# Hybrid attention and HGRN2 block: all attention values in one job of 512 columns, and two other jobs moved forward

## The chip, the core and the metric

The kernel runs on one core of a Trainium2 chip. The time is device microseconds of one launch: the median of three runs of the kernel before is 1435.72 us (1435.06 to 1435.78). Five engines with queues of their own work side by side: TensorE (PE in the profile, with its weight loads as PEld), VectorE (DVE), ScalarE (ACT), GpSimd (POOL) and SyncE (SP), which issues most of the DMAs. Each executes its list of instructions in order and waits for the others where a tile demands it.

## The reference

One layer on x of 1024 tokens by 1024 columns, in float32. After an RMS norm, one projection `w_in` gives everything that the two branches need:

```python
xn = rmsnorm(x, norm1_g[layer])
u = xn @ w_in[layer].astype(f32)
q_sb, k_sb, v_sb, f_raw, i_hg, q_hg, g_hg, gate_sb, gate_hg = jnp.split(u, list(c), axis=-1)
o_sb = stick_breaking_attention(split_heads(q_sb, SB_HEADS), ...)      # 8 heads of 64
f = lb + (1.0 - lb) * jax.nn.sigmoid(f_raw)
k_hg = (1.0 - lb) * jax.nn.sigmoid(-f_raw)
o_hg = hgrn2_chunkwise(silu(q_hg), k_hg, i_hg, log(f))                 # 4 heads of 128
o_hg = rmsnorm(o_hg, hg_norm_g) * jax.nn.silu(g_hg)
merged = g_a * (o_sb @ w_o_sb) + g_b * (o_hg @ w_o_hg)                 # g_a, g_b: sigmoids of the gates
h = x + merged @ w_out
h = h + jnp.square(jax.nn.relu(rmsnorm(h, norm2_g) @ w_ff1)) @ w_ff2
return rmsnorm(h, final_g)
```

Stick-breaking attention is strictly causal: the weight of key s for query t is sigmoid(z_ts) times the product of (1 - sigmoid(z_tj)) over the keys j between s and t. HGRN2 is a linear recurrence over tokens, S_t = diag(f_t) S_(t-1) + k_t v_t, with the output S_t' q_t.

## The kernel before, in words

**Products.** Every float32 product is made of three matmuls on pairs: an operand is split into hi (a rounded copy, by ScalarE as a CAST) and lo (the rest, by VectorE as a subtraction, L161); `three` (L553) issues hi by hi, hi by lo and lo by hi into one PSUM bank. A `Unit` holds one piece of weights: `load` fetches it, `split` makes hi and lo.

**Jobs and lanes.** Projections are jobs of a `Stream` (`st`, L487): a job is a list of steps of a few matmuls, in the order in which the jobs were added. `st.advance(n, upto)` issues n further steps, but none beyond job `upto`; `st.finish(upto)` issues all up to there. Starting a job also splits the next one's weights and loads those of the one after it. TensorE's instructions lie on two lanes, "main" (the steps of the attention and of HGRN2, which depend on other engines) and "fill" (the stream's steps). Within these orders a scheduler places the instructions of each engine, in view of the pools of tiles (`slots` of 1024 columns, `halves` of 512, raw and split weights, eight PSUM banks).

**Stages.**
1. Head: norm of x and transposes to `xn` (`xnt`) in two halves of tokens, among them the first job (`first_job`, L728), which makes q and k of head 0 (`pjqk`) and V of heads 0 to 3 (`pjv0`), 256 columns wide, one piece for each of eight token blocks.
2. Attention: 64 items, eight heads by eight query blocks in the order 7, 0, 6, 1, 5, 2, 4, 3. Each item has scores (`z`, TensorE, then two sigmoids on ScalarE), weights (a scan and a product on VectorE, tiles `rm` and `bt`, L802 and L169), a turn (`pw`, transposes of the weights, split to hi and lo) and values (`po`). After each item the stream goes on by its share of `n_fill` = 126 steps, up to job `j_att`. The jobs are q and k of heads 1 to 7, V of heads 4 to 7 (`v_job(1)`, behind head 4), f and q of the HGRN2 heads (`pjf`, `pjq`), and two raw output-gate jobs (`raw_job`, KT and KT+1).
3. HGRN2: for each of four heads `hg_levels(h)` (L1006), which yields eight times, and `hg_tail(h)` (L1131), six times; the tail of head h-1 runs in turns with the levels of head h. In the levels, VectorE makes products of k and q (the pair sums `sd`, `sl` of levels 0 and 1, through `pairs_of` and `sums_of`), multiplies k and q by the decay of a level (tile `pp`), and lays the scores of a level (`sl`) into `sc` with predicated copies (L1051, L1122). Levels 2 to 4 take their scores from k and q in 16 matmuls, levels 5 and 6 in many small ones. The tail transposes k (`pk`), makes the states (`pkv`, and a chain of seven updates of k on VectorE, L1159 and L1161), the outputs (`pho`), their norm (squares on ScalarE, a power on POOL, a product `hon` on VectorE) and transposes (`pot`).
4. The gates (`gX`, `gY`: TensorE's products with summed operands `gs`), the output product, the MLP.

The loop of stage 3, where the order of the fill is set:

```python
    FILL = (3.4, 2.2, 2.8, 2.9, 2.9)
        upto = (j_i, j_raw[1], j_raw[6], j_sb[1], j_sb[2])[h]
                if next(g, StopIteration) is not StopIteration:
                    owed += FILL[h]
                    st.advance(int(owed), upto)
                    owed -= int(owed)
```

`upto` is a job: the fill of head 0 goes up to the job of i (`pji`), that of head 3 up to the second, and the last turn's (h = 4, only the tail of head 3) up to the third of the four jobs `j_sb`, the products of the attention's output with `w_o_sb` (`pys`). What is left of these is finished behind the loop.

Of the kernel before, what the change touches and what calls it, by code (L numbers as in the profile page):

```python
# [9 lines left out]
F32 = mybir.dt.float32  # L10
F32R = mybir.dt.float32r
# [8 lines left out]
P = 128  # L20
T = 1024
# [18 lines left out]
def kernel(  # L40
# [86 lines left out]
    def matmul(*a, **k):  # L127
        return pe(nc.tensor.matmul(*a, **k))  # L128
# [449 lines left out]

    def token_steps(name, unit, acts, tbs, epilogue, lo_last=False, n=256):

        pk = 1024 // n
        for tb in tbs:
            ps = bank(f"{name}_{tb}")[:, 0:n]
            for lo in (False, True) if lo_last else (None,):
                for kt in range(KT):
                    sh, sl = acts.stat(kt, tb)
                    wh, wl = unit.hl[kt // pk]
                    cs = slice((kt % pk) * n, (kt % pk + 1) * n)
                    if lo is None:
                        three(ps, sh, sl, wh[:, cs], wl[:, cs], kt == 0, kt == KT - 1)  # L590
                        if kt < KT - 1 and kt % pk == pk - 1:
                            yield
                    elif lo:
                        matmul(ps, sh, wl[:, cs], start=False, stop=kt == KT - 1)
                    else:
                        matmul(ps, sh, wh[:, cs], start=kt == 0, stop=False)
                        matmul(ps, sl, wh[:, cs], start=False, stop=False)
                if lo is False:
                    yield
            epilogue(ps, tb)  # L600
            yield

    def wide_unit(name, mat, c0, n=256):
# [56 lines left out]

    def v_epilogue(quad):


        def ep(ps, tb):
            if tb % 2 == 0:
                vt[quad, tb // 2] = slot(f"V{quad}_{tb // 2}", F32R)
            V = vt[quad, tb // 2].rearrange("p (t h s d) -> p t h s d", t=2, h=4, s=2)
            src = ps.rearrange("p (h d) -> p h d", h=4)
            hi_lo(V[:, tb % 2, :, 0, :], V[:, tb % 2, :, 1, :], src)

        return ep

# [4 lines left out]
    def qk_epilogue(h):  # L677
# [12 lines left out]
        return ep  # L690

    def v_unit(quad):
        return wide_unit(f"wv{quad}", W_IN, C_V + quad * 256)

    def v_job(quad):
        unit = v_unit(quad)
        return st.add(
            [unit], lambda: token_steps(f"pjv{quad}", unit, xn, range(NT), v_epilogue(quad))
        )

# [27 lines left out]
    def first_job():  # L728
        name, u_qk, ep = qk_item(0)
        u_qk.__class__ = FirstUnit  # L730
        u_v = v_unit(0)

        def body():
            v_ep = v_epilogue(0)
            for half, parts in enumerate((((0, 2), (2, 2)), ((0, 4),))):
                ps = bank(f"{name}_{half}")
                for b0, n in parts:
                    ts = slice(b0 * P, (b0 + n) * P)
                    yield from proj_half(ps[:, ts], u_qk.hl[0], xn.mov, KT, half, ts=ts)
                    if b0 + n == 4:  # L740
                        ep(ps, half)
                    if half == 0 and b0 > 0:
                        st.prefetch()
                    tb = 4 * half + b0
                    yield from token_steps("pjv0", u_v, xn, range(tb, tb + n), v_ep, tb == 0)

        return st.add([u_qk], body), u_qk, u_v

    j_first, u_qk0, u_v0 = first_job()
# [256 lines left out]
    def hg_levels(h):  # L1006
# [16 lines left out]

        def pairs_of(name, n, *products):

            t, h_, l_ = (slot_n(f"{name}_{x}", n, d) for x, d in zip("xhl", (F32, F32R, F32R)))
            for (a, b, w), (i, cs) in zip(products, halves()):
                x = mul(t[:, cs].rearrange("p (n c) -> p n c", c=w) if w else t[:, 0:n], a, b)
                after(x, turn_lo[0] if "sd0" in name else None)
            return name, n, h_, l_, x, hi_lo(h_, l_, t)  # L1030

        def sums_of(pairs):

            name, n, h_, l_ = pairs[:4]
            open_block("main")
            banks = []
            for c0 in range(0, n, 512):
                S = bank(f"{name}_{c0}")
                matmul(S, ones, h_[:, c0 : c0 + 512], start=True, stop=False)
                matmul(S, ones, l_[:, c0 : c0 + 512], start=False, stop=True)  # L1040
                banks.append(S)
            return banks
# [15 lines left out]

        pairs = pairs_of(f"sd{h}", T, (k, q, 0))
        for _, cs in halves():  # L1060
            after(mul(q[:, cs], q[:, cs], dec[:, cs]), pairs[4])
        if h == 0:
            u_i.split(1)
        yield
        for l in range(7):
# [5 lines left out]
            if l == 0:  # L1071
                pairs = pairs_of(
                    f"sl{h}_{l}", 512, (blocks_of(k, 1)[:, :, 0, 0], blocks_of(q, 1)[:, :, 1, 0], 0)
                )
                if h == 0:
                    u_i.split(2)
            elif l == 1:
                if h == 0:
# [3 lines left out]
                    f"sl{h}_{l}",  # L1082
                    T,
                    *((kv[:, :, i : i + 1].to_broadcast([P, T // 4, 2]), qv, 2) for i in (1, 0)),
# [26 lines left out]
            elif l == 1:  # L1111
                if h == 0:
                    diagonal(first_sums, pairs[4])
                after(lay(masks[0], sums[0], 1), pairs[5] if h == 0 else None)
            elif l == 2:
                for m, S in zip(masks[-2:], sums):
                    lay(m, S, 2)
# [1139 lines left out]
    st.advance(4, 1)  # L2257
    u_v0.split()
    norm1((2, 3))
    st.advance(3, 1)  # L2260
    norm_transpose(xn, 0, 2, 2)
    st.advance(5, 1)
    norm1(range(4, NT))
    st.advance(4, 1)
    norm_transpose(xn, 1, 0, 4)
    turns["on"] = False
    turn_vectors(1, 6)
    lower_bounds()
    make_masks()
    st.advance(11, j_qk[0])  # L2270
    scores(*items[0])
    weights(*items[0])
    st.advance(1, j_qk[0])
    scores(*items[1])
    st.finish(j_qk[0])

    n_fill = 9 * (j_q[1] - 1 - j_qk[0]) + 7 + 7 + 4
    n_first = 3
    ready = deque()
# [154 lines left out]
```

## Time and profile before

| | |
|---|---|
| median of three runs | 1435.72 us (1435.06 to 1435.78) |
| profiled execution | 1435.25 us |
| its span | 1433.4 us |
| TensorE busy | 1423.1 us (99%), 7248 matmuls |
| VectorE busy | 1118.9 us (78%) |
| ScalarE busy | 675.5 us (47%) |
| DMA | 233.57 MB, mean 163 GB/s |

The span goes from the first to the last thing recorded on the core; the execution's own time has 1.85 us around it. Stages in this execution: head until about 49 us, attention until about 303 us, HGRN2 until about 569 us, then gates, output product and MLP. A row of a timeline has a start, a duration, the engine, the line of the kernel, the operation, out<-in, and the number of instructions it stands for. The duration of a VectorE row includes an end that overlaps the next instruction, so the spacing of starts is what an instruction takes of the engine.

### The profile page before, as it was taken

To read this page: it belongs to the slowest core of one execution; us is meant where nothing else is said; L and a number is where in the kernel's file an instruction comes from. 1 tells how busy PE (TensorE), PEld (TensorE's weight loads), DVE (VectorE), ACT (ScalarE), POOL (GpSimd) and SP (SyncE) were. 2 spreads that over 40 slices of the span, in tenths; PEclk is the share of its full clock that TensorE was granted. 3 is DMA by queue.
4 is the path that set the end of the run, shared out by engine and by line. 5 is a ranking of instruction groups with operands and counts; after the bars stand their busy time and mean duration, and the time that the engine had idled before them with its cause. 6 is when DMAs were issued, how large, how long until landed. Compare 5 with 4: busy or idle time off the path is not lost.

```text
span 1433.4 us, 19568 instructions
## 1 busy us (share of the span) xinstructions
PE 1423.1 (99%) x7248; PEld 1205.2 (84%) x7248; DVE 1118.9 (78%) x1525; ACT 675.5 (47%) x1165; POOL 141.3 (10%) x338
## 2 busy tenths in 40 slices
PE   9999999999999999999999999999999999999998
PEld 8989988888888888888888888888888888888886
DVE  6799899998567888798787897666666758668765
ACT  7566666653143444433344674544444433524343
POOL 3121132200011031000000300000000000000032
PEclk9999999999999999999999999999999999999999
DMA  7235154542025775555476405434446974776725
GB/s 214 48 93 132 31 109 68 126 111 74 16 56 159 249 183 191 164 167 187 138 281 241 176 31 198 145 138 141 157 156 219 343 269 157 272 276 241 278 98 186
DMA packets 162359, 233.57 MB, mean 163 GB/s; under 512 B 26028, under 2 KB 95192, under 8 KB 162264
## 3 DMA queue, kind: packets, MB, share of 16 engines
q1 hardware_dynamic: 146424, 190.11, 39.3%
q0 software_dynamic: 11520, 34.61, 9.2%
q10 hardware_dynamic: 4320, 7.60, 1.4%
q8 instruction: 57, 0.93, 0.3%
q14 instruction: 38, 0.31, 0.1%
HBM read 167.27 MB, written 65.01 MB: 162 GB/s over the span
## 4 chain that ended last, share of the span: by engine, by line
PE 95%; DVE 2%; issue 1%; ACT 1%; POOL 1%; DMA 0%; SPq 0%; DVEq 0%; POOLq 0%; ACTq 0%
PE pm L128 21%; PE pX L128 9%; PE pW L128 6%; PE pY L128 6%; PE pjqk L128 6%; PE gX L128 4%; PE gY L128 4%; PE pga L128 4%; PE pys L128 3%; PE pji L128 3%; PE pyh L128 3%; PE pjf L128 3%; PE sl L128 2%; PE pjv L128 2%; PE po L128 2%; PE pjq L128 2%
## 5 line engine op out<-in xcount | busy, mean ns | idle before, releaser
L156 ACT CAST whid<-w 128x1024 fp32r<-128x1024 f32 x30 | 31.6, 1054 | 154.3 <-PE pm L128 85.9
L802 DVE TENSOR_TENSOR_SCAN rm<-rm,bits 128x511 f32<-128x511 f32 (+7 forms) x72 | 87.5, 1219 | 11.1 <-ACT rm L780 10.8
L128 PE MATMUL pm<-whid,sh 128*128 128x512 f32 x240 | 93.4, 389 | 0.0
L128 PE MATMUL pm<-wlod,sh 128*128 128x512 f32 x240 | 93.4, 389 | 0.0
L128 PE MATMUL pm<-whid,sl 128*128 128x512 f32 x240 | 93.4, 389 | 0.0
L128 PE MATMUL pm<-tl,sh 128*128 128x512 f32 (+1 forms) x210 | 81.3, 387 | 0.0
L128 PE MATMUL pm<-th,sl 128*128 128x512 f32 (+1 forms) x210 | 81.3, 387 | 0.0
L128 PE MATMUL pm<-th,sh 128*128 128x512 f32 (+1 forms) x210 | 81.3, 387 | 0.0
L161 DVE TENSOR_TENSOR wlod<-w,whid 128x1024 fp32r<-128x1024 f32 x30 | 36.7, 1224 | 55.9 <-ACT whid L156 55.9
L161 DVE TENSOR_TENSOR sl<-sa,sh 128x1024 fp32r<-128x1024 f32 x56 | 68.3, 1219 | 0.1
L156 ACT CAST wTh<-pw 128x512 fp32r<-128x512 f32 (+2 forms) x96 | 44.0, 484 | 47.6 <-PE pw L131 47.1
L156 ACT CAST sh<-sa 128x1024 fp32r<-128x1024 f32 x56 | 57.2, 1046 | 6.9 <-DMA sa<-ad 6.9
L2072 POOL TENSOR_SCALAR fss<-fss 128x1 f32<-128x1 f32 x8 | 4.4, 552 | 562.1 <-ACT fsc L2067 561.6
L161 DVE TENSOR_TENSOR wTl<-pw,wTh 128x512 fp32r<-128x512 f32 (+2 forms) x96 | 50.6, 548 | 3.5 <-ACT wTh L156 3.1
L128 PEld LDWEIGHTS pm<-whid,sl 128*128 128x128 f32 x240 | 45.1, 188 | 9.3
L128 PEld LDWEIGHTS pm<-wlod,sh 128*128 128x128 f32 x240 | 45.0, 188 | 9.4
L128 PEld LDWEIGHTS pm<-whid,sh 128*128 128x128 f32 x240 | 45.1, 188 | 9.3
L169 DVE TENSOR_TENSOR bt<-bt,rm 128x511 f32<-128x511 f32 (+7 forms) x72 | 49.2, 686 | 4.0
L780 ACT ACTIVATE rm<-z 128x511 f32<-128x511 f32 (+4 forms) x96 | 48.0, 501 | 4.5 <-DVE g L169 1.8
L128 PE MATMUL pX<-sql,t1h 128*128 128x512 f32 x128 | 50.0, 391 | 0.1
L128 PE MATMUL pX<-sqh,t1l 128*128 128x512 f32 x128 | 49.8, 389 | 0.0
L128 PE MATMUL pX<-sqh,t1h 128*128 128x512 f32 x128 | 49.8, 389 | 0.0
(939 smaller groups left out, 4526.7 us busy)
## 6 DMA issues: line engine op xcount, KB each, us to landing
w<-in_w_ff_dram SPq DMA_DIRECT2D x72, 512.0 KB, 4.8
sa<-ad SPq DMA_DIRECT2D x56, 512.0 KB, 6.7
ad<-a SPq DMA_DIRECT2D x32, 256.0 KB, 2.0
ad<-s SPq DMA_DIRECT2D x16, 512.0 KB, 6.8
tw<-in_w_out_dram POOLq DMA_DIRECT2D x24, 256.0 KB, 3.8
pr<-pd SPq DMA_DIRECT2D x10, 512.0 KB, 6.2
x<-in_x_dram SPq DMA_DIRECT2D x8, 512.0 KB, 8.8
xnl<-xnh POOLq DMA_DIRECT2D x8, 512.0 KB, 8.2
```

What stands on the lines that cost most here:

```text
L128: return pe(nc.tensor.matmul(*a, **k))
L156: hi_last[0] = after(in_turn("act", nc.scalar.copy(dst, src)), hi_behind[0])
L161: nc.vector.tensor_tensor(out=dst, in0=src, in1=hi.bitcast(F32), op=ALU.subtract),
L169: return nc.vector.tensor_tensor(out=out, in0=a, in1=b, op=ALU.mult)
L780: nc.scalar.activation(rm[:, s0 + c0 - 1 : s0 + m - 1], z[:, c0:m], AF.Sigmoid, scale=-0.125)
L802: sc = nc.vector.tensor_tensor_scan(out=rr, data0=rr, data1=bits[:, 1024 - nk + a : 1024 - nk + b][:, ::-1], initial=rm[:, b : b + 1] if i ...
L2072: nc.gpsimd.tensor_scalar(out=ssq, in0=ssq, scalar1=1.0 / D, scalar2=EPS, op0=ALU.mult, op1=ALU.add)
```

## The change

1. V of all eight heads is made in the first job, 512 columns wide (`wv`, `pjv`), from four pieces of weights in place of two; `v_job(1)` is gone. The first two token blocks take the hi products of the first pieces first.
2. `q_job(0)` and `raw_job(KT)` come behind head 4's q and k, where `v_job(1)` was. `f_job(2)`, the forget gates of the third HGRN2 head, comes ahead of `q_job(2)` and the job of i, and is now the last job within the attention (`j_att`). `n_fill` is 126 as before.
3. In the levels, `pairs_of` and `sums_of` use two tiles of 512 columns in place of one of 1024.
4. In the head, the four pieces of V's weights are loaded ahead of x4 to x7, and the steps between the norms are spread anew.

`FILL` and `upto` in the loop of HGRN2 are unchanged. The core of the diff:

```diff
@@ token_steps
-    def token_steps(name, unit, acts, tbs, epilogue, lo_last=False, n=256):
+    def token_steps(name, unit, acts, tbs, epilogue, n):
...
@@ values of the attention
-    def v_epilogue(quad):
-        def ep(ps, tb):
+    def v_epilogue(ps, tb):
+        for quad in range(2):
             if tb % 2 == 0:
                 vt[quad, tb // 2] = slot(f"V{quad}_{tb // 2}", F32R)
             V = vt[quad, tb // 2].rearrange("p (t h s d) -> p t h s d", t=2, h=4, s=2)
-            src = ps.rearrange("p (h d) -> p h d", h=4)
+            src = ps[:, quad * 256 : (quad + 1) * 256].rearrange("p (h d) -> p h d", h=4)
             hi_lo(V[:, tb % 2, :, 0, :], V[:, tb % 2, :, 1, :], src)
...
@@ first_job
-        u_v = v_unit(0)
+        u_v = wide_unit("wv", W_IN, C_V, 512)
+        u_v.roomy = range(4)
+        open_banks = {}
+
+        def v_part(tb, kt, hi=True, lo=True):
+            if kt == 0 and hi:
+                open_banks[tb] = bank(f"pjv_{tb}")
+            ps = open_banks[tb]
+            sh, sl = xn.stat(kt, tb)
+            wh, wl = (w[:, kt % 2 * 512 : (kt % 2 + 1) * 512] for w in u_v.hl[kt // 2])
+            if hi:
+                matmul(ps, sh, wh, start=kt == 0, stop=False)
+                matmul(ps, sl, wh, start=False, stop=False)
+            if lo:
+                matmul(ps, sh, wl, start=False, stop=kt == KT - 1)
+
+        def v_steps(tb, kts):
+            for kt in kts:
+                v_part(tb, kt)
+                if kt == KT - 1:
+                    v_epilogue(open_banks.pop(tb), tb)
+                if kt % 2 == 1:
+                    yield
...
         def body():
...
+            ps = bank(f"{name}_0")
+            yield from qk_steps(ps, 0, 0, 2)
+            for hi in (True, False):
+                for k0 in (0, 2):
+                    for tb in range(2):
+                        for kt in (k0, k0 + 1):
+                            v_part(tb, kt, hi, not hi)
+                    yield
+            yield from qk_steps(ps, 0, 2, 2)
+            ep(ps, 0)
+            st.prefetch()
+            for tb in range(4):
+                yield from v_steps(tb, range(4, KT) if tb < 2 else range(KT))
+            ps = bank(f"{name}_1")
+            yield from qk_steps(ps, 1, 0, 4)
+            ep(ps, 1)
+            for tb in range(4, NT):
+                yield from v_steps(tb, range(KT))
...
-    for h in range(1, NHS):
-        j_qk[h] = proj_jobs([qk_item(h)], xn)
-        if h == 4:
-            v_job(1)
...
@@ hg_levels
-        def pairs_of(name, n, *products):
+        def pairs_of(name, *products):
-            t, h_, l_ = (slot_n(f"{name}_{x}", n, d) for x, d in zip("xhl", (F32, F32R, F32R)))
-            for (a, b, w), (i, cs) in zip(products, halves()):
-                x = mul(t[:, cs].rearrange("p (n c) -> p n c", c=w) if w else t[:, 0:n], a, b)
+            his, los = [], []
+            for i, (a, b, w) in enumerate(products):
+                t, h_, l_ = (
+                    slot_n(f"{name}_{x}{i}", 512, d) for x, d in zip("xhl", (F32, F32R, F32R))
+                )
+                x = mul(t.rearrange("p (n c) -> p n c", c=w) if w else t, a, b)
                 after(x, turn_lo[0] if "sd0" in name else None)
-            return name, n, h_, l_, x, hi_lo(h_, l_, t)
+                his.append(h_)
+                los.append(l_)
+                lo = hi_lo(h_, l_, t)
+            return name, his, los, x, lo
...
@@ order of the jobs
+    for h in range(1, NHS):
+        j_qk[h] = proj_jobs([qk_item(h)], xn)
+        if h == 4:
+            q_job(0)
+            raw_job(KT)
     f_job(0)
-    q_job(0)
-    raw_job(KT)
     f_job(1)
     q_job(1)
-    j_att = raw_job(KT + 1)
+    raw_job(KT + 1)
+    f_job(2)
+    j_att = j_f[2]
     q_job(2)
     j_i = i_job()
-    f_job(2)
     f_job(3)
     q_job(3)
...
@@ loads and head
     u_qk0.load()
-    u_v0.roomy = (1,)
-    u_v0.load(1)
+    u_v.load(1)
     load_x(2)
-    u_v0.load()
-    for tb in range(3, NT):
+    u_v.load(2)
+    load_x(3)
+    u_v.load()
+    for tb in range(4, NT):
         load_x(tb)
...
-    n_fill = 9 * (j_q[1] - 1 - j_qk[0]) + 7 + 7 + 4
-    n_first = 3
+    n_fill = 9 * (NHS - 1 + 5) + 7 + 7 + 4
+    n_first = 4
```

More of the change, by code (lines that the diff above doesn't have):

```diff
@@ L583, in token_steps @@
             ps = bank(f"{name}_{tb}")[:, 0:n]
[L584 to L598, printed above, removed]
+            for kt in range(KT):
+                sh, sl = acts.stat(kt, tb)
+                wh, wl = unit.hl[kt // pk]
+                cs = slice((kt % pk) * n, (kt % pk + 1) * n)
+                three(ps, sh, sl, wh[:, cs], wl[:, cs], kt == 0, kt == KT - 1)
+                if kt < KT - 1 and kt % pk == pk - 1:
                     yield
@@ L690, in qk_epilogue @@
         return ep
[L692 to L699, printed above, removed]
     def qk_item(h):
@@ L730, in first_job @@
         u_qk.__class__ = FirstUnit
-        u_v = v_unit(0)
-        def body():
[L734 to L745, printed above, removed]
+        u_v = wide_unit("wv", W_IN, C_V, 512)
@@ L1057, in diagonal @@
                 after(mul(chunks(sc[:, cs]), chunks(sums[i]), over_chunks(ident)), behind)
-        pairs = pairs_of(f"sd{h}", T, (k, q, 0))
+        pairs = pairs_of(f"sd{h}", *((k[:, cs], q[:, cs], 0) for _, cs in halves()))
         for _, cs in halves():
-            after(mul(q[:, cs], q[:, cs], dec[:, cs]), pairs[4])
+            after(mul(q[:, cs], q[:, cs], dec[:, cs]), pairs[3])
         if h == 0:
@@ L1112, in hg_levels @@
                 if h == 0:
-                    diagonal(first_sums, pairs[4])
-                after(lay(masks[0], sums[0], 1), pairs[5] if h == 0 else None)
+                    diagonal(first_sums, pairs[3])
+                after(lay(masks[0], sums[0], 1), pairs[4] if h == 0 else None)
             elif l == 2:
@@ L2257 @@
     st.advance(4, 1)
-    u_v0.split()
+    u_v.split(2)
     norm1((2, 3))
```

30 lines of the change are left out of this document (16 added, 14 removed).

## The prediction

> **What bounds the kernel now.** I read the page first (busy shares, the forty slices, the chain), then the waits of TensorE, then windows by stage, and last the timelines of the places that the change touches.
>
> ```profile
> span 1433.4 us, 19568 instructions
> ...
> PE 1423.1 (99%) x7248; PEld 1205.2 (84%) x7248; DVE 1118.9 (78%) x1525; ACT 675.5 (47%) x1165; POOL 141.3 (10%) x338
> ...
> PE 95%; DVE 2%; issue 1%; ACT 1%; POOL 1%; DMA 0%; SPq 0%; DVEq 0%; POOLq 0%; ACTq 0%
> ```
> ```profile
> PE warm L128 <- POOL ident masks.py:199: 2.2, 1, 2.2
> PE xnt L131 <- DVE x L640: 0.3, 1, 0.3
> PE pjqk L128 <- DVE xnl L339: 0.3, 1, 0.3
> PE z L128 <- DVE q L169: 0.2, 1, 0.2
> ```
> TensorE is 99% busy, its four waits come to 3.0 us, and the chain is 95% TensorE. So a microsecond of matmul taken away is a microsecond gained, and every new wait of TensorE is lost in full: 1423 us of work leave no place in which to make it up.
>
> Three windows, one of the attention and two of the HGRN2 stage (columns: length, then busy time and count of PE, PEld, DVE, ACT and POOL, clock, DMA share, GB/s), show how near the second engine is:
>
> ```profile
> 49.00:285.00 236.00, 235.80 (x1436) 208.69 (x1435) 214.92 (x307) 157.07 (x351) 50.70 (x178) 1.00 0.39 89
> ...
> 303.12:343.13 40.01, 40.01 (x209) 34.13 (x208) 37.27 (x50) 16.82 (x26) 1.15 (x2) 1.00 0.44 139
> 530.61:568.21 37.60, 37.60 (x233) 31.71 (x232) 31.79 (x47) 18.60 (x38) 6.13 (x9) 1.00 0.62 186
> ```
> VectorE works 215 of 236 us in the attention, 37.3 of 40 in head 0's levels, 31.8 of 37.6 at the end of head 3. TensorE stays full only because jobs of other work ("fill") are spread between its dependent steps. The change moves exactly that fill.
>
> **The V job at 512 columns.**
>
> ```profile
> 148.11 2.87 PE pjv L128 x24
> ...
> 569.78 2.75 PE gX L128 x12
> ...
> 597.01 2.72 PE gX L128 x12
> ```
> Before, V is 384 matmuls of 256 columns, at 2.87/24 = 0.1196 us. After, it is 192 of 512 columns, at 2.72/12 = 0.227 (the same kind of three-part product, nearest in form), or 0.229 by the first gX row. 384 x 0.1196 = 45.9; 192 x 0.227 = 43.5, or 44.0. I take **-2.4 us**, with -1.9 as the other end. Over the whole change VectorE gets 12 instructions more and ScalarE 8, because V's evictions and the pair sums go by halves; the bytes stay, and TensorE's fill covers them.
>
> **The head.** Another 1 MB of V weights goes through SP's queue ahead of x4 to x7.
>
> ```profile
> GB/s 0 33 201 393 380 290 248 266 349 405 363 384 409 410 401 414 414 396 240 127 223 210 256 46 0 8 0 0 0 70 70 29 126 221 200 95 1 0 0 0
> ...
> 29.83 3.65 PE L131 MATMUL xnt<-ident,x 128*128 128x128 f32 x32
> ...
> 28.38 0.75 DVE L655 TENSOR_SCALAR x<-x,n_y 128x1024 f32<-128x1024 f32 x1 [0.72 <-POOL n_y L257]
> ```
> The first row has one value for each microsecond from 0. At about 400 GB/s 1 MB takes 2.6 us, so x7 arrives that much later, and the qk weights queued behind it on SP too (needed only when V is done). But the second half's transposes (x32) now stand behind 48 wide V matmuls, 10.9 us, in place of 48 narrow ones, 5.7, so some 5 us later on TensorE. The norm that ends at 29.1 has that room. Cost taken: **+0.3 us** (the V steps ahead of the third block's transposes are a little shorter); ends 0 and 2.6, the whole transfer.
>
> **Attention.** There the fill is exchanged: V's second job, 17 steps, goes out and f2 comes in, in a budget of 126 steps as before; q0 and one raw gate job only change places. From the first scores to head 0's first pair sums TensorE has 264 us of work in the changed order, by the spacings above and their like, against 267. VectorE's 9% of slack there isn't touched: f2's splits and evictions are of the size of the second V job's. I cost the exchange at nothing, the cover being that fill (up to +2 if VectorE's slack is unevenly spread), but for the last block, where the list of fill now ends. Between z of query block 3 and its transposed weights TensorE has 2.05 us left of other work; before, it had this:
>
> ```profile
> 301.07 0.40 PE L128 MATMUL z<-KS,QL 128*128 128x512 f32 x1
> ...
> 301.70 0.60 ACT L780 ACTIVATE rm<-z 128x511 f32<-128x511 f32 x1
> ...
> 303.12 1.22 DVE L802 TENSOR_TENSOR_SCAN rm<-rm,bits 128x511 f32<-128x511 f32 x1
> 304.45 0.69 DVE L169 TENSOR_TENSOR bt<-bt,rm 128x511 f32<-128x511 f32 x1
> ...
> 309.06 0.60 PE L131 MATMUL pw<-ident,bt 128*128 128x128 f32 x4
> ```
> The chain takes 0.6 + 1.33 + 0.69 = 2.6, with two hand-overs some 2.9 us: **+0.8** (0 to 1.5).
>
> **Head 0 of HGRN2.** Before, f2 is part of the fill between these levels; now it is gone, and after z of block 3 TensorE has 30.4 us of work up to level 4's scores (sl), by the rows' spacings. VectorE must do 49 operations between, from that scan to level 3's product of q. Spacings from these rows:
>
> ```profile
> 326.47 0.69 DVE L169 TENSOR_TENSOR q<-q,pp 128x512 f32<-128x512 f32 x1
> 327.08 1.22 DVE L161 TENSOR_TENSOR sl_l<-sl_x,sl_h 128x1024 fp32r<-128x1024 f32 x1
> 328.21 1.22 DVE L161 TENSOR_TENSOR wil<-wir,wih 128x1024 fp32r<-128x1024 f32 x1
> ...
> 331.68 1.29 DVE L1051 COPY_PREDICATED sc<-masks,sl 128x512 f32<-128x512 uint8 x1
> 332.76 1.25 DVE L161 TENSOR_TENSOR wf2l<-wf2r,wf2h 128x1024 fp32r<-128x1024 f32 x1
> ...
> 339.98 1.98 DVE L1122 COPY_PREDICATED sc<-masks,sl 128x512 f32<-128x512 uint8 x3
> 341.83 0.69 DVE L169 TENSOR_TENSOR k<-k,pp 128x512 f32<-128x512 f32 x1
> 342.43 0.70 DVE L169 TENSOR_TENSOR q<-q,pp 128x512 f32<-128x512 f32 x1
> ...
> 343.66 1.61 PE L128 MATMUL sl<-q,k 128*128 128x128 f32 x13
> ```
> Next starts give 0.61 us for 512 columns, 1.13 for 1024, 1.08 and 0.62 for the two predicated copies. In the changed order: 29 of 512 (17.7), 6 of 1024 (6.8), two long and three short copies (2.2 + 1.9), the scan (1.3) and 8 small ones, halves and quarters of a 512 (2.6): 32.5 us. To that comes 0.9 until the scan starts and 0.7 for a lo part that waits for its hi copy on ScalarE: 34.1 against 30.4. Before, the scan to this product is 40.0 us of time, and level 4's scores start 0.5 us after it: already at the edge. So **+3.7 us** here, felt at level 3's scores (some 1.5) and level 4's, the 0.8 above apart. Ends: 0 (VectorE hands over sooner than spacings say) and 5. Heads 1 and 2 keep a microsecond and more at each level; nothing is counted for them.
>
> **Head 3's end.** f2 was done earlier, so the fill list runs out earlier too. Head 3's loop wants 2.9 steps after each of 14 yields, 41, and finds 36 up to its limit; before, it found them all. The last loop, which wants 17, finds 9 where it had 14. In the changed order level 6's scores are followed at once by the transposes of k, and the last outputs (pho), both output transposes (pot) and the first gate product (gX) stand one behind the other. From level 4's last scores to the last pot TensorE has 84 matmuls of 512 columns and small ones: 84 x 0.227 + 4.6 = 23.6 us. Before, it had this:
>
> ```profile
> 529.58 0.38 PE L128 MATMUL sl<-q,k 128*128 128x128 f32 x2
> ...
> 541.28 1.15 PE L128 MATMUL sl<-q,k 128*64 128x64 f32 x16
> ...
> 546.57 0.93 PE L131 MATMUL pk<-ident,k 128*128 128x128 f32 x7
> ...
> 563.03 0.39 PE L128 MATMUL pho<-k,q 128*128 128x128 f32 x2
> ...
> 569.18 0.60 PE L131 MATMUL pot<-ident,hon 128*128 128x128 f32 x4
> ...
> 560.77 0.34 DVE L1161 SCALAR_TENSOR_TENSOR k<-k,fc,pkv 128x128 f32<-128x128 f32 x1
> 561.03 1.22 DVE L161 TENSOR_TENSOR wlog<-wg8r,whig 128x1024 fp32r<-128x1024 f32 x1
> ...
> 567.52 0.69 DVE L169 TENSOR_TENSOR hon<-pho,hn_y 128x512 f32<-128x512 f32 x1 [0.93 <-POOL hn_y L257]
> ```
> Between level 4's product of k and the last hon VectorE has 46 operations in the changed order: 16 of 1024 (18.1), 18 of 512 (11.0), a predicated copy (0.6), six state steps (0.26 each, by the next start: 1.6), five tiny ones (0.7): 32.0 us, without a wait. So at least 8.4 us of TensorE's time go. The waits lie in series with it: by the same spacings TensorE waits 0.3 at level 6's scores, 3 at the transposes of k, 1.5 in the first pho, 4.5 in the second. Then the last pot waits for squares on ScalarE, a power on POOL and hon: from the last pho row's start to hon's start the rows give 567.52 - 563.03 = 4.5 us, some of it another cast, so 3 to 4 more. Sum **+12.5 us**, ends 8.4 and 14.5. Nothing later waits less for it: TensorE has no idle time to give back there.
>
> **Sum.** -2.4 + 0.3 + 0.8 + 3.7 + 12.5 = +14.9. The profiled execution took 1435.25 us (its span 1433.4, and 1.85 around it), the median is 1435.72, 0.47 above. 1435.25 + 14.9 = 1450.2; against the median it is about the same (1450.6). I forecast **1450 us**, slower by 1.0%. What can be told from no change is about 0.2%, 2.9 us.
>
> **The rivals.**
> *Only the V saving (not slower).* Head 3's end was never bound by VectorE, if the work counted there isn't due before the pot: 1435.25 - 2.4 + 0.3 = 1433.2, and 1432.6 at the best price. It decides from the point where the 32.0 us of VectorE fit into 23.6: over 8 us of these 46 operations, half of the 16 wide ones, would have to be done before. For it: the wide ones are splits of gates and weights, whose data are there early. Against it: VectorE works in its listed order, and they are listed between the products that TensorE needs. Chance 0.08.
> *Head 0 hides its gap.* If VectorE is ahead when z of block 3 comes, the 4.5 of head 0 go and head 3's stay: 1435.25 - 2.4 + 0.3 + 12.5 = 1445.7. For it: my lead there rests on hand-overs of a microsecond; chance 0.25.
> *TensorE's clock falls in the new gaps.* At the cold start this kernel shows
>
> ```profile
> 2.25 4.27 PE L128 MATMUL warm<-ident 128*128 128x128 f32 x20 [2.25 <-POOL ident masks.py:199]
> ...
> 8.59 1.31 PE L131 MATMUL xnt<-ident,x 128*128 128x128 f32 x10
> ```
> 0.213 us for each of twenty matmuls against 0.13 for later transposes of the same size, so a cold TensorE is at little more than half speed for about 4 us. If a gap of 3 to 4 us does this again at head 3's end, some 2 us are lost, twice at most 4: 1452 to 1454. Chance 0.2; no gap of that length is in the trace. The Trainium skill, "TensorE: Matmul & The Clock Gate", Part 1 ("What's actually happening"), says that the clock halves after an idle window of about 3.4 us and takes about as long of steady work to come back; the slow start agrees (twenty matmuls in 4.3 us), the fall after a gap is in no run here, and my waits of 3 to 4.5 us, cut by small matmuls, lie on either side of it.
> *The head's loads are late.* The whole 2.6 us of transfer come through: 1452.5; chance 0.05, since the room of 4.8 us would have to be gone.
>
> **Chances.** My sum as it stands (1447 to 1452) 0.42; head 0 hidden 0.25, clock 0.2, loads 0.05, V saving only 0.08. The range is 1441 to 1456: below, the lower ends of head 0 (0) and head 3 (8.4) together, 1435.25 - 2.4 + 0.3 + 8.4 = 1441.6; above, head 3's upper end (+2), head 0's (+2) and 2 of cold clock. The V saving alone lies at the edge of what can be told, so its 0.08 is halved: faster 0.04, within 0.2% 0.04, slower 0.92.
>
> **What would show it.** Of the changed profile: pjv as x12 groups of 2.7 us in place of x24 of 2.87; waits of TensorE behind VectorE's q or k (level 3 and 4 of head 0), and about ten more at head 3, with pk behind k, pho behind the state's k, and pot behind hon as the largest; TensorE's busy time lower by 2 to 3 us while the span grows; VectorE 95% or more busy in the stretch from level 4 of head 3 to its last hon; the first gX some 12 us later than V's saving alone would put it. The forecast is wrong if these 46 operations show gaps, so that TensorE's work and not VectorE's set that stretch, or if TensorE's waits at head 0 are below 2 us in sum.

## The result, and the profile after

The changed kernel takes 1451.46 us (median of four, 1451.42 to 1451.79) against 1435.63 us: 1.0111 times the time before, 95% interval 1.0099 to 1.0124. The forecast was 1450 us in a range of 1441 to 1456. The profiled execution took 1451.45 us, its span is 1449.7, 16.3 us more than before.

The page of the changed kernel, and its waits of TensorE (engine, what waited, for whom: us in total, times, longest):

```profile
span 1449.7 us, 19206 instructions
...
PE 1429.0 (99%) x7056; PEld 1197.9 (83%) x7056; DVE 1118.8 (77%) x1537; ACT 676.5 (47%) x1173; POOL 142.5 (10%) x338
```
```profile
PE pot L131 <- DVE hon L169: 2.5, 1, 2.5
PE pho L128 <- DVE k L1172: 2.3, 3, 1.2
PE warm L128 <- POOL ident masks.py:199: 2.2, 1, 2.2
PE pk L131 <- DVE k L169: 2.0, 1, 2.0
PE pga L128 <- DVE q L169: 1.3, 1, 1.3
PE pw L131 <- DVE bt L169: 1.0, 1, 1.0
PE sl L128 <- DVE q L169: 0.9, 2, 0.7
```
Before, four waits came to 3.0 us, 2.2 of them at the start. Now the ten others make about 11 us. 6.8 lie at head 3's end (pot, pho, pk), where the fill ran out; the last two rows are the attention's last block (`pw`) and, for 0.7 of its 0.9, head 0 (`sl`); the one at `pga` is in the middle of the attention, where I had expected none. The rest, not shown, are short ones in the head and one of 0.3 us at `po`.

The waits don't make up the whole loss. The chain, in order of time, shows V and the first gate products (start, duration, operation, count):

```profile
62.58 10.91 PE pjv L128 x48
...
583.48 4.88 PE gX L128 x12
588.36 2.75 PE gY L128 x12
...
748.86 21.76 PE pwW L128 x96
```
V's matmuls of 512 columns take 10.91/48 = 0.227 us as expected. But the first gX takes 4.88 us for what takes 2.75 a moment later. TensorE's clock says why (windows: length, then busy time of PE, PEld, DVE, ACT, POOL with counts, clock, DMA share, GB/s):

```profile
543.90:582.20 38.30, 31.33 (x200) 25.74 (x198) 33.56 (x49) 18.41 (x38) 4.89 (x8) 0.94 0.47 159
572.50:577.60 5.10, 2.79 (x16) 2.08 (x15) 4.16 (x8) 2.22 (x8) 1.52 (x2) 1.00 0.35 133
577.60:588.20 10.60, 8.06 (x27) 6.31 (x27) 4.68 (x7) 4.28 (x12) 1.20 (x2) 0.52 0.54 164
```
From 572.5 on TensorE is 55% busy for 5 us, and then the granted clock is about half (0.52) for 10.6 us. So the largest part of the change's price is what stands in the first of these windows: 38.3 us for head 3's end, and a slow start of the gates after it.

To see how much is lost in which stage I use four marks, the first product of head 1's q and k, head 0's first pair sum (`sd`), the first gX and the first pwW (733.01 us before). From the time at a mark TensorE's listed work up to it is taken off, with the same duration for a matmul form in every kernel, and then the same difference of the kernel before. What is left is what the stage lost. For the changed kernel: head 0.7 us, attention 4.2, HGRN2 11.1, gX 2.3; together 18.4 before rounding, of which V's shorter work pays 2.6 by the same count. The same count gives TensorE's work in the attention, from the first product of head 1's q and k on: 254.6 us, against 266.8 before.

### The profile page after: what moved, and what is told of

Same layout as the page of the kernel before. It is cut to its first block, busy times and chain, and to the rows that moved or that the text cites. A ratio compares the mean times of both kernels' runs of the same rounds, so it can differ in the third digit from the quotient of the medians.

```text
span 1449.7 us, 19206 instructions
## 1 busy us (share of the span) xinstructions
PE 1429.0 (99%) x7056; PEld 1197.9 (83%) x7056; DVE 1118.8 (77%) x1537; ACT 676.5 (47%) x1173; POOL 142.5 (10%) x338
## 4 chain that ended last, share of the span: by engine, by line
PE 94%; DVE 3%; ACT 1%; issue 1%; POOL 1%; DMA 0%; ACTq 0%; DVEq 0%; POOLq 0%
PE pm L128 21%; PE pX L128 9%; PE pW L128 6%; PE pY L128 6%; PE pjqk L128 5%; PE gX L128 4%; PE pga L128 4%; PE gY L128 4%; PE pyh L128 3%; PE pys L128 3%; PE pjf L128 3%; PE pjv L128 3%; PE po L128 2%; PE z L128 2%; PE pjq L128 2%; PE pji L128 2%
## 5 line engine op out<-in xcount | busy, mean ns | idle before, releaser
L789 ACT ACTIVATE bt<-z 128x512 f32<-128x512 f32 (+3 forms) x96 | 47.9, 501 | 4.9 <-DMA od<-osb 2.6
```

What stands on the lines that cost most here:

```text
L789: nc.scalar.activation(bt[:, s0 : s0 + e], z[:, :e], AF.Sigmoid, scale=0.125)
```

## The experiments

The parts of the change are tried by themselves first: f2's place, V's width, the pair sums in halves. Then come the limits of the fill, the clock, and the attention.

**f2 back (e1_f2_back).** The changed kernel with one part undone.

```diff
     q_job(1)
-    raw_job(KT + 1)
-    f_job(2)
-    j_att = j_f[2]
+    j_att = raw_job(KT + 1)
     q_job(2)
     j_i = i_job()
+    f_job(2)
     f_job(3)
...
-    n_fill = 9 * (NHS - 1 + 5) + 7 + 7 + 4
+    n_fill = 9 * (NHS - 1 + 4) + 7 + 7 + 4
```


> The changed kernel with one part undone: head 2's forget gates (f2) behind the job of i again, where they were before, and the budget of the attention 9 steps smaller (117). V stays one wide job. Theory (the time is lost because f2's 10.9 us of TensorE work are missing as fill at head 3's end): the waits at pk, pho and pot (8.4 us in the changed profile) and the slow first gX (2.6 us) go, while the attention, which now has 10.9 us less of fill, waits for VectorE some 1 to 5 us more; 1441 to 1445 us. Rival (the wide V job and its later blocks cost it, wherever f2 is): no gain, 1449 us or more. If the attention has room for all, 1438 to 1440.

Measured 1440.84 us, 10.6 less than the changed kernel and 0.2 below the theory's range. Its largest waits, the one at the start apart:

```profile
PE po L128 <- DVE wTl L161: 1.7, 2, 1.3
PE pw L131 <- DVE bt L169: 1.3, 1, 1.3
PE sl L128 <- DVE q L169: 0.6, 1, 0.6
```
Nothing is left at pk, pho and pot, and the clock stays at 1.00. The attention lost 5.5 us instead of 4.2: f2 was of use there, but its place costs 12 us in the later stages (13.4 lost there against 1.6).

**f2 forward, V narrow (e2_f2_forward).** The other half, on the kernel before, with the pair sums in halves.

```diff
-    j_att = raw_job(KT + 1)
+    raw_job(KT + 1)
+    f_job(2)
+    j_att = j_f[2]
     q_job(2)
     j_i = i_job()
-    f_job(2)
```


> The kernel before, narrow V in two jobs, with f2 moved into the attention (and the pair sums in halves of 512, without which the tiles don't fit). Theory: the tail of head 3 is bare as in the changed kernel; waits at pk, pho and pot of 8 to 9 us and a slow gX of 2 to 3 us, 1445 to 1448 us. Rival (the wide V is what costs): 1435 to 1438 us, with no waits at head 3.

Measured 1448.77 us, 0.8 above the theory's range. Three of its waits:

```profile
PE pot L131 <- DVE hon L169: 2.5, 1, 2.5
PE pho L128 <- DVE k L1166: 2.3, 3, 1.2
...
PE pk L131 <- DVE k L169: 2.0, 1, 2.0
```
The three waits are those of the changed kernel to a tenth, with V still in two narrow jobs. So it is f2's place that bares head 3's end. In the attention this kernel loses nothing. What lifts it above the range is a second fall of the clock, which the changed kernel does not have: at `pk`, about 1.5 us by the spacings of the rows there (shown in the last section).

**Pair sums in halves alone (e5_before_halves).** The kernel before with the changed `pairs_of` and `sums_of`.

```diff
-        pairs = pairs_of(f"sd{h}", T, (k, q, 0))
+        pairs = pairs_of(f"sd{h}", *((k[:, cs], q[:, cs], 0) for _, cs in halves()))
```


> The kernel before with only the pair sums in two tiles of 512 columns. Theory: nothing that can be told, 1435 to 1437 us. Rival (the halves make VectorE's chain at levels 0 and 1 of each head longer): waits at sd and sl, 1438 us or more.

1436.21 us against 1435.82 beside it, one run each: no part of the loss that can be told.

**V early but narrow (e13_v_early).** Is it V's width that costs in the attention, or that all of V is done ahead of it? V's second narrow job comes directly behind the first and is finished there.

```diff
     j_qk = {0: j_first}
-    for h in range(1, NHS):
-        j_qk[h] = proj_jobs([qk_item(h)], xn)
-        if h == 4:
-            v_job(1)
+    j_v1 = v_job(1)
...
+    for h in range(1, NHS):
+        j_qk[h] = proj_jobs([qk_item(h)], xn)
+        if h == 4:
+            q_job(0)
+            raw_job(KT)
     f_job(0)
-    q_job(0)
-    raw_job(KT)
     f_job(1)
...
-    st.finish(j_qk[0])
...
+    st.finish(j_v1)
...
-    n_fill = 9 * (j_q[1] - 1 - j_qk[0]) + 7 + 7 + 4
...
+    n_fill = 9 * (NHS - 1 + 4) + 7 + 7 + 4
```
(The pair sums are in halves here too.)

> The kernel before (with pair sums in halves) with V narrow, 256 columns in two jobs, but the second job directly behind the first, ahead of head 1's q and k, and so finished before the attention's paced fill begins; q0 and raw KT where the changed kernel has them, f2 behind the job of i as before, the attention's budget 117 steps. It is the run with f2 back, but for V's width. Theory (the 4 to 5 us that the attention loses with wide V come from where V's work stands: all of it early, and none left as fill between the later heads): the same attention waits, and 2.4 us more of matmuls, less 0.7 of the head: 1442 to 1443 us. Rival (the width costs them, through the eight wide evictions or their banks): the attention as free as before, only head 0's waits of 2.6 us stay, 1437 to 1438.5 us.

1445.78 us, above even the theory's range, and far from the rival's. The waits of the run with f2 back are there again, at the same places:

```profile
PE po L128 <- DVE wTl L161: 2.1, 3, 1.3
PE pw L131 <- DVE bt L169: 1.4, 1, 1.4
```
The attention lost 8.0 us here. So the place is what costs; the width is not needed for it. About 1.6 us of the difference to 5.5, by the spacings of the rows, is a fall of the clock after the longest wait (last section); the rest I can't assign. The place of q0 and raw KT is not told apart from V's: in every kernel with V early these two jobs stand behind head 4 as well. What the runs do show is how much work is left for the attention. From the first product of head 1's q and k on, TensorE has 277.7 us in the run with f2 forward and narrow V, 266.8 in the kernel before, 254.6 in the changed kernel and 243.7 in the two runs with V early and f2 back; 0, 0, 4.2, and 5.5 and 8.0 us are lost.

The four by stage, in us lost against the kernel before (by the marks above), and the times:

| | head | attention | HGRN2 | gX | time |
|---|---|---|---|---|---|
| V late, f2 forward (e2) | 0.2 | 0.0 | 11.5 | 1.9 | 1448.77 |
| V early and narrow, f2 back (e13) | 0.8 | 8.0 | 1.6 | 0.0 | 1445.78 |
| V early and wide, f2 back (e1) | 0.8 | 5.5 | 1.6 | 0.0 | 1440.84 |
| V early and wide, f2 forward (changed) | 0.7 | 4.2 | 11.1 | 2.3 | 1451.46 |

**Limits one job further (e3_limits).** There is other work that can cover head 3's end: the last `j_sb` job, which stands among the gates.

```diff
-        upto = (j_i, j_raw[1], j_raw[6], j_sb[1], j_sb[2])[h]
+        upto = (j_i, j_raw[1], j_raw[6], j_sb[2], j_sb[3])[h]
```


> The changed kernel with the limits of head 3's fill and the last turn's one job further (the third and fourth of the jobs j_sb in place of second and third), so that the work of the fourth job, 10.9 us that now stands among the gate products, covers head 3's end. Theory: the waits there and the slow gX go, 11 us, 1440 to 1441 us, and the gates, which have the fill no more, stay full. Rival (VectorE's work sets the stretch through the gates too): the waits move to the gate products, gX and gY, 1445 to 1451 us.

1444.86 us, between the theory and the rival: 6.6 of the 11 us. The old waits are gone, and there is one new one:

```profile
PE pkv L128 <- ACT pp L1155: 3.4, 1, 3.4
```
It isn't at the gate products, where the rival put it. TensorE waits for ScalarE's copy of the transposed k (`pp`). That copy overwrites the tile of decay factors, out of which VectorE must first take the last ones (`fc`, 0.17 us). VectorE, then ScalarE:

```profile
562.01 0.17 DVE L169 TENSOR_TENSOR pp<-pp 128x8 f32<-128x8 f32 x1
...
568.30 1.22 DVE L1239 TENSOR_TENSOR gs<-xnl,gs 128x1024 f32<-128x1024 f32 x1
569.44 0.17 DVE L1146 COPY fc<-pp 128x8 f32<-128x8 f32 x1
```
```profile
569.55 1.05 ACT L156 CAST gsh<-gs 128x1024 fp32r<-128x1024 f32 x1 [2.61 <-DVE gs L1239]
570.50 0.96 ACT L1155 COPY pp<-pk 128x512 f32<-128x512 f32 x2
```
The factors were ready at 562.2, but in VectorE's list `fc` now stands behind 7 us of splits and sums for the gates. In the changed kernel the same copy waits 2.50 us for `fc`, and TensorE still has fill in that time. The cast ahead of `pp` on ScalarE adds at most 0.9 us, from the end of `fc` to the start of `pp`. So the moved fill job also moved the order of VectorE's list, and a copy of 0.17 us came late. The wait also brought a fall of the clock, 1.7 us by the spacings behind it.

**The last turn's limit alone (e6_last_turn).**

```diff
-        upto = (j_i, j_raw[1], j_raw[6], j_sb[1], j_sb[2])[h]
+        upto = (j_i, j_raw[1], j_raw[6], j_sb[1], j_sb[3])[h]
```


> The changed kernel with the limit of the last turn alone moved on, to the fourth of the jobs j_sb; head 3's own limit stays, so the fill still runs out at level 6 but is there again from the second pho on. Theory: the wait at pk (2 us) stays, those in the second pho go for the most part (3.3 to about 1) and the one at the last pot (2.5) and the slow gX (2.6) go whole; 1451.5 - 2.3 - 2.5 - 2.6 = 1444 us. Rival (as soon as the fill comes back VectorE or ScalarE, which both still have the gates' work in their lists, set the end): 1447 us or more, with another wait of 3 us or so as at pkv in the run with both limits moved.

1444.48 us, as forecast, but partly by luck: the wait of 2.0 us at pk is still there, 0.5 is left in the second pho (1 was forecast), none at the pot, and the first gX is quick. Here the clock fell at pk, however, which the theory did not have: the granted clock is half for 3.4 us from 558.1 on, 1.6 us by the spacings.

**Idle matmuls in the waits (e4_warm, e9_warm_half).** Is the slow gX the clock's doing? Matmuls without use are put into the waits, to keep TensorE busy.

```diff
             pk = bank(f"pk{h}_{half}")
+            if h == 3 and half == 0:
+                keep_warm_in(pk, 16)
...
+                if h == 3 and half == 1 and j < 3:
+                    open_block("main")
+                    keep_warm_in(po, (3, 9, 5)[j])
+                    open_block("main")
                 matmul(po[:, js], sc[:, cs], v[:, cs], start=True, stop=c == 0)
...
             pot = bank(f"pot{h}_{half}")
+            if h == 3 and half == 1:
+                keep_warm_in(pot, 20)
```


> The changed kernel with 53 idle matmuls of 128 columns (the identity by itself, into columns that are written over later) put into the waits at head 3's end: 16 ahead of pk, 17 among the second pho, 20 ahead of the last pot; some 5.7 us of work at full clock, in waits of 8.4 us. They add nothing to the result. Theory (the first gX is slow because the clock falls when TensorE is mostly idle for some microseconds): gX takes 2.75 us again in place of 4.88, the granted clock is 1.00 in that stretch, and the time is 2 to 3 us lower, 1448.5 to 1449.5 us. Rival (gX is slow for a reason of its own, its operands or its bank): gX 4.9 us as before and 1451 us or more.

1451.44 us, above the theory's range, and yet the clock was 1.00 throughout and gX took 2.75 us: each float32 matmul shows as two records, so that the 53 were 11.5 us of work in place of 5.7, and overfilled the waits by as much as the clock gave back. The second kernel has 8, (1, 5, 3) and 11 of them.

> The changed kernel with idle matmuls in head 3's waits as in the run before, but half as many (8 ahead of pk, 9 among the second pho, 11 ahead of the last pot), because each of them took two passes of 0.11 us there and the 53 overfilled the waits by 3 us. 28 of them take 6.1 us of the 8.4. Theory (the clock's fall is worth the 2.3 us that gX grew, and the rest of that stretch too): no added time by the matmuls, gX in 2.75 us, 1448.5 to 1449.3 us. Rival (what is won at the clock is only bought with the time of the idle matmuls): 1451 us.

1448.26 us, 0.2 below the theory's range. Where the clock had fallen the rows now read (timeline of TensorE: start, duration, then as before):

```profile
555.90 2.05 PE L128 MATMUL pk<-ident 128*128 128x128 f32 x16
...
578.71 2.62 PE L128 MATMUL pot<-ident 128*128 128x128 f32 x22
581.83 0.66 PE L131 MATMUL pot<-ident,hon 128*128 128x128 f32 x4 [0.50 <-DVE hon L169]
...
583.00 0.40 PE L128 MATMUL gX<-gsh,whig 128*128 128x512 f32 x1
583.24 0.39 PE L128 MATMUL gX<-gsl,whig 128*128 128x512 f32 x1
```
The next starts of gX are 0.23 us apart (0.43 in the changed kernel). Work that does nothing makes the kernel 3.2 us faster; that is about the price of the fallen clock (one run), 2.3 of it in gX by the marks, the rest probably in the small products ahead of it, which the window of half clock holds too.

**The fill spread anew (e7_even, e10_raw0_forward).** If bare places are all that costs, a better spread must win it back.

```diff
-    n_fill = 9 * (NHS - 1 + 5) + 7 + 7 + 4
+    n_fill = 9 * (NHS - 1 + 5) + 7 + 7 + 4 - 8
...
-    FILL = (3.4, 2.2, 2.8, 2.9, 2.9)
+    FILL = (3.4, 2.2, 2.8, 2.4, 3.4)
...
-        upto = (j_i, j_raw[1], j_raw[6], j_sb[1], j_sb[2])[h]
+        upto = (j_i, j_raw[1], j_raw[6], j_sb[1], j_sb[3])[h]
```


> The changed kernel with its fill spread anew: eight steps fewer in the attention's budget (118), the rates 2.4 and 3.4 steps for head 3 and the last turn, and the last turn's limit at the fourth of the jobs j_sb. By the order of its instructions TensorE now has 8 us between z of block 3 and its turn (2.05 in the changed kernel), 40 us up to level 4 of head 0 (30.4), and fill at every step of head 3's end. Theory (bare places are all that costs): head 0's 2.7 us, head 3's 8.7 us and the clock's 2.6 us go, 1451.5 - 14.0 = 1437.5 us; up to 2 more for the 5 us of fill that the attention gives up, 1437.5 to 1439.5. Rival (VectorE's list is too full in the attention to spare eight steps): waits of 4 to 5 us there, 1442 us.

1440.27 us (1438.69 to 1440.73), 1.0029 times the kernel before (1.0018 to 1.0041). The median lies between the theory and the rival. HGRN2 loses 0.5 us and gX nothing, but the attention 6.2 in the profiled execution (1440.54 us) in place of 4.2. About 1.6 of this, by the spacings, is again a fall of the clock, at 169.6 us. It probably doesn't come each time: the four executions with a mean granted clock of 0.997 or 0.998 took 1440.27 to 1440.73 us, the three with 0.999 took 1438.69 to 1438.98, inside the theory's range. Without the fall the attention would lose about 4.6, so the eight steps cost it little by themselves, but they bring it to the edge of a fall (TensorE 47% busy in the 3.4 us before it; see the last section). A difference of 1.7 us between single runs of two kernels, e1 and e13 among them, can be this alone.

The next one gives the attention seven more steps, the first of the raw gate jobs, and leaves them for the last block:

```diff
     f_job(2)
-    j_att = j_f[2]
+    j_raw = [raw_job(0)]
+    j_att = j_raw[0]
...
-    j_raw = [raw_job(cb) for cb in range(KT)]
+    j_raw += [raw_job(cb) for cb in range(1, KT)]
...
-    n_fill = 9 * (NHS - 1 + 5) + 7 + 7 + 4
+    n_fill = 9 * (NHS - 1 + 5) + 7 + 7 + 7 + 4 - 7
...
-    FILL = (3.4, 2.2, 2.8, 2.9, 2.9)
+    FILL = (3.4, 2.2, 2.5, 2.3, 2.9)
```
(with the limit of e7_even)

> The changed kernel with the first of the eight raw gate jobs moved into the attention too, behind f2, its seven steps left over at the attention's end as cover for the last block; rates 2.5, 2.3 and 2.9 for heads 2, 3 and the last turn; the last turn's limit at the fourth of the jobs j_sb. Theory: no waits at the last block's turn, at head 0, at head 3's end and no slow gX (15.5 us of the changed kernel's loss), the attention's other waits (some 2.7 us) and the head's 0.7 stay, 1435.7 - 2.4 + 3.4 = 1436.5 us. Rival (fill taken from the later stage is missed there): 1440 us or more, with the waits among the gates.

1437.64 us (1437.27 to 1438.69), 1.0016 times the kernel before (1.0007 to 1.0026), 1.1 above the theory. Apart from the one of 2.2 us at the start, its largest waits are:

```profile
PE pga L128 <- DVE q L169: 1.2, 1, 1.2
PE pjqk L128 <- DVE xnl L339: 0.3, 1, 0.3
```
13.8 of the 15.8 us are won back with the change's V, f2 and halves kept. The kernel before is still the faster: the attention's 2.8 us, HGRN2's 0.9 and the head's 0.7 are more than the 2.4 that wide V saves.

**The wait at pga (e11_raw_later, e12_raw_first).** Two tries on that kernel to be rid of it, with the job raw KT elsewhere.

```diff
         if h == 4:
             q_job(0)
+        if h == 5:
             raw_job(KT)
```


> The run with the first raw gate job forward, and besides the job raw KT behind head 5's q and k in place of behind q0. In the changed kernel TensorE waits 1.4 us at the first matmul of raw KT for VectorE's product q, which frees its bank, right behind q0. Theory (this wait is of that neighbourhood): it goes, 1.4 us less than the run with the first raw gate job forward. Rival (VectorE is behind at that place whatever follows): a wait of the same size at another matmul there, the same time within 0.5 us.

```diff
         if h == 4:
+            raw_job(KT)
             q_job(0)
-            raw_job(KT)
```


> The same with raw KT ahead of q0. Theory: as in the run with raw KT later, 1.4 us less than with the changed order. Rival: the raw job's larger share of VectorE comes earlier and only moves the wait, the same time within 0.5 us.

1437.68 and 1438.53 us, one run each. For the first the rival holds; the second is 0.9 above the run that it starts from, outside the rival's 0.5, but within the spread of that run's ten executions. Neither gains what the theory said. In the first the wait of 1.2 is replaced by 0.7 at po, 0.4 at pw and 0.3 at pjqk, in the second by 1.0 at z and 1.0 at pgq, each of them for VectorE. It is behind there, and the two other orders of jobs only change who waits for it.

## Why the prediction was right

Right were the sign, the size (14.9 us forecast, 15.8 measured) and the place: head 3's end, because f2's steps are missing there, as e1 and e2 show from both sides. Of the two signs that it had named for being wrong, one came whole and one in part (head 0 and VectorE's gaps, below), so the size is better than the steps behind it. By its steps:

- *V at 512 columns, -2.4.* By the chain's row 192 x 0.227 = 43.6 against 45.9: -2.3. Right.
- *Head, +0.3.* 0.7 measured; within its ends.
- *Attention, nothing but the last block's 0.8.* This step failed: 4.2 us, of which about 1.5 at the last block's `pw` and `po`. It compared sums from the first scores on, 264 us of TensorE's work against 267, and by the spacings of the records they are indeed about equal (273 and 270). What it didn't ask is where in the stage the work stands. Of the 273 us, 16 are V's, which is over before the paced fill begins; in the kernel before, half of V came behind head 4 at the pace of the rest. From head 1's q and k on it is 254.6 us against 266.8, so 12 us of cover were gone. The upper end of 2 us, which I gave for VectorE's 9% of slack being uneven, was too low.
- *Head 0, +3.7 from a gap of 34.1 against 30.4.* 1.1 measured at `sl` by the spacings, 0.7 of it in the list of waits. This is the first sign: waits below 2 us at head 0 were to show the forecast wrong, and this step was. *Head 3's end, +12.5 from 32.0 against 23.6.* About 9 measured without the clock (the waits of 6.8, 0.3 at level 6's scores, and short ones). Both have the same mis-sized term: TensorE's small products, which I took from the program's list at one pass each ("84 x 0.227 + 4.6"). The row quoted in the prediction itself, sixteen records of `sl` at level 6 in 1.15 us, where the list has eight matmuls, says that each is two passes. For levels 2 to 4, too, 16 is the number of records of one level, and the list has eight matmuls. The records follow each other by 0.032 us at 32 columns, 0.058 at 64 and 0.11 at 128. With these the second passes of levels 5 and 6, pkv and both pho are 3.4 us more at head 3's end, and those of two levels' scores 1.8 us more in head 0. With that the steps give 9.1 and 1.9.
- *VectorE without a gap in the 46 operations of head 3's end.* This is the second sign, and it came in part: VectorE shows gaps of 1.3, 0.2, 0.9 and 2.3 us there. Only the first is for TensorE (`pys`), the last two are for POOL's power ahead of hon. It is 33.6 of 38.3 us busy, 88%, not 95%: the end is a chain that passes between engines, with VectorE as its longest part.
- *The clock, a rival with 0.2.* It did fall. 3.2 us by e9, in the 2 to 4 that I gave. My waits of 3 to 4.5 us were too long, the longest that came were 2.0 to 2.5, and it fell all the same, behind the three in the second pho (2.3 us together).
- *Other rivals.* V's saving alone is excluded by the waits (its lower figure, 1432.6, is 1432.9 by its own terms), late loads by the head's 0.7 us. Head 0 hidden holds in part: of its 4.5 us, last block included, about 2.6 came.
- *The first gX some 12 us later than by V's saving alone.* This counts head 3 alone; the whole sum says 17, and 16 were measured.

So the sum was right partly by luck: about 6 us too much at heads 0 and 3, 5 of them the passes, stood against 3 too little in the attention and 3 of clock. TensorE's busy time was to fall by 2 to 3 us and rose by 5.9; a slower clock counts as busy, which is some 3 us of it, and what the rest is I haven't settled.

## What to carry to other kernels

Where one engine is full only because filler work lies between its dependent steps, a job that is moved earlier is paid for where it was taken from: look for the place where the filler list now ends, and set there the other engines' listed work against what is left. Compare it step by step and not by the sum of a stage, and take durations of small products from records in a trace, not from the count in a program. A saving of 2.4 us of matmul is worth nothing as long as the work that it shortens was also the cover of something. And look at VectorE's list as well as TensorE's after a job is moved: a copy of 0.17 us that came late made TensorE wait 3.4 us.

## What the runs showed of the hardware

The clock fell after shorter waits than I thought. Two places where it did, with the wait and the first slow rows; first in the run with f2 forward and narrow V, where one wait of 2.0 us did it:

```profile
554.85 1.76 PE L131 MATMUL pk<-ident,k 128*128 128x128 f32 x7 [2.02 <-DVE k L169]
556.26 0.78 PE L128 MATMUL pys<-asbh,wo02h 128*128 128x512 f32 x1
556.83 0.63 PE L128 MATMUL pys<-asbl,wo02h 128*128 128x512 f32 x1
```
and in the run with V early and narrow, about 1 us after waits of 0.5 and 1.3 us:

```profile
172.79 0.38 PE L128 MATMUL po<-wTl,V 128*128 128x256 f32 x1 [1.31 <-DVE wTl L161]
...
174.38 0.63 PE L128 MATMUL z<-KS,QH 128*128 128x512 f32 x1
```
The spacing of 512 columns is 0.43 us in place of 0.23 until 557.7 and 177.2 us, some 3 us in each. The same wait of 2.0 us at pk in the changed kernel had no such effect; in the run with the last turn's limit alone it had.

What decides is where the wait falls. In every trace kept here the granted clock changes only at instants that lie whole multiples of 3.41 us apart. Here are the stretches between such instants (columns as in the windows of the first section): around the wait at pk and up to the fall in the changed kernel; then at pk in the run with f2 forward and narrow V; then the least busy one that had no fall, in the run with f2 back:

```profile
553.82:557.23 3.41, 2.14 (x21) 1.51 (x19) 3.24 (x5) 3.17 (x5) 0.00 (x0) 1.00 0.02 7
557.23:560.64 3.41, 2.40 (x14) 2.14 (x15) 3.41 (x6) 1.14 (x2) 0.00 (x0) 1.00 0.20 77
574.30:577.71 3.41, 1.55 (x11) 1.17 (x11) 2.79 (x5) 0.62 (x1) 0.59 (x1) 1.00 0.20 77
577.71:581.12 3.41, 2.12 (x9) 1.45 (x8) 1.62 (x4) 2.05 (x10) 0.74 (x2) 0.50 0.73 235
```
```profile
551.03:554.44 3.41, 1.54 (x18) 1.01 (x16) 3.24 (x5) 2.74 (x5) 0.00 (x0) 1.00 0.00 0
```
```profile
167.06:170.47 3.41, 1.87 (x13) 1.68 (x14) 3.31 (x6) 1.66 (x6) 0.13 (x2) 1.00 0.57 120
```
In the changed kernel the wait at pk is shared by two stretches, in which TensorE is 63% and 70% busy, and the clock stays. With f2 forward and narrow V it lies in one, 45% busy, and the clock is halved at its end. All 14 traces, divided in this way, agree. The clock fell at the end of every stretch at full clock in which TensorE was at most 48% busy: seven inside the kernels, at 16% to 48%, and those at the kernels' ends. It fell after none at 55% or more. It came back after a stretch at half clock that was 88% busy or more, and not after one of 73% or less, so that a fall lasted 3.4 us in five cases and 10.2 in two. So the same wait can cost 1.5 us or nothing, as it falls. The shares are the profile's; where between 48% and 55% the bound lies isn't shown.

The Trainium skill, "TensorE: Matmul & The Clock Gate", Part 1 ("What's actually happening"), says that the windows over which activity is judged run free, so that the turning point varies; the stretches here, which begin at another place in each run, agree with that. It gives an idle window of about 3.4 us as what halves the clock; here windows in which TensorE was up to 48% busy did, and the measurement decides.

Unexpected for me was also that a float32 matmul of 128 columns takes two records of 0.11 us each, as the idle matmuls showed (8 listed, 16 recorded, 2.05 us with the slower first one and the end of the last).
